# Spare words between the tile pools of a DiT block on one core: the same instructions at other SBUF addresses

## The chip, the core and the metric

The kernel runs on one core of one Trainium2 chip. TensorE (PE in the profile) multiplies; it reads both operands from SBUF and writes to PSUM. VectorE (DVE), ScalarE (ACT) and GpSimd (POOL) prepare operands and empty PSUM, and DMAs queued by SyncE (SP) bring weights from HBM. The metric is the device time of one execution in microseconds: 1252.46 us before (median of 3 runs, 1251.32 to 1253.43).

## What is computed

Two layers of a diffusion transformer over 512 latent tokens and 256 context tokens, 1024 wide. Layer 0 mixes tokens by pooling over windows, layer 1 by grouped-query attention (8 heads, 4 of keys and values). Each layer ends in a squared-ReLU MLP of width 4096. Cut to what matters:

```python
for i in range(DEPTH):                       # 2 layers
    sh1, sc1, g1, sh2, sc2, g2 = split(s_lat @ ada_w[i] + ada_b[i], 6)
    a_l = modulate(rms_norm(h_lat, norm_g[i, 0]), sh1, sc1)
    ...
    y_l = pool_mix(a_l, ...) if kind == 0 else attn_mix(a_c, a_l, ...)
    h_lat = h_lat + g1 * y_l
    m_l = modulate(rms_norm(h_lat, norm_g[i, 1]), sh2, sc2)
    h_lat = h_lat + g2 * (square(relu(m_l @ mlp_w1[i])) @ mlp_w2[i])
    ...                                      # the context alike in layer 0
return rms_norm(h_lat, final_g)
```

## The kernel before

**Arithmetic.** All large products are fp32r matmuls. To keep precision, each operand is split into a rounded part and the rest (`hilo`, L91 and L92: ACT copies the rounded part, DVE subtracts it from the source), and a product is three matmuls: high by high, high by low, low by high. A matmul has a *streamed* operand (256 or 512 columns of 4 bytes pass through the array) and *weights* (128 x 128, loaded before it; the profile calls the load PEld). The weights of the next matmul are loaded while the one before streams.

**Stages and lines.** Pooling and its mix (L641, L668); MLP of layer 0 over 16 chunks of 256 hidden columns; attention (projections L889, scores L967 and L968, values L998, output L1009); MLP of layer 1. In an MLP chunk the first product is either plain (`m1_chunk`, L376) or, from chunk 5 of layer 0 and chunk 4 of layer 1 on, by Strassen's scheme with seven half-sized products of 256 columns (`m1_strassen`, L444; its part for the context is L464). The second product is `m2_chunk`, L495: for each of 8 output blocks, six matmuls with 512 latent columns, and in layer 0 six with 256 context columns between them. So 14 chunks of layer 0 give 672 pairs of one 512-column and one 256-column matmul. Adaptive-norm parameters of layer 1 are summed by L232.

**Order.** The scheduler and two hand-ordered stretches set each engine's order; every engine works its queue in that order and waits by semaphores. The program is fully unrolled.

**Where tiles lie.** Pools are laid out in SBUF in the order in which they are opened, each tile rounded up to 32 bytes, one after another. What begins 32 bytes past a multiple of 128 at the start of a pool stays there for all its tiles, since the tiles are multiples of 128 bytes long and all slices that matmuls read start at multiples of 512 bytes. The table gives for each pool what matmuls read from it, and its start modulo 128 in the built program, before and after the change:

| pool | tiles that matmuls read | before | after |
| --- | --- | --- | --- |
| `const` | `ident`, `ones` | 0 | 0 |
| `big` | `act`, `m_hi`, `m_lo` (`a_m_hi`, `a_m_lo` in attention), `h_ctx` (also spare weights of Strassen in layer 1) | 32 | 0 |
| `wp` | `w`: weights, and streamed by the projections L889 | 32 | 32 |
| `mc` | `m_c`, `a_c`, attention's `q` and `o`, Strassen weights of layer 1 | 96 | 64 |
| `xs` (both layers) | `xs`: sums streamed by Strassen | 96 | 64 |
| `op` (layer 0) | `op`: Strassen weights | 96 | 32 |
| `kvp` | `k` (streamed), `v` (weights) | 96 | 32 |

So before, `act` and `w` are 0 apart modulo 128, as are `m_hi` and `w`, `xs` and `op`; `m_c` and `w`, `m_hi` and `op`, `act` and `v` are 64 apart. The pairs are read off the table the same way for any product.

Of the kernel before, what the change touches and what calls it, by code (L numbers as in the profile page):

```python
# [8 lines left out]
F32 = mybir.dt.float32  # L9
# [5 lines left out]
P = 128  # L15
# [32 lines left out]
def dit_block_kernel(ctx: ExitStack, tc: tile.TileContext, xT, cols, adab, adaw, w1, w2, wqkv, wo,  # L48
# [4 lines left out]
    def sb(stack, name, bufs):  # L53
        return stack.enter_context(tc.tile_pool(name=name, bufs=bufs))

    const = sb(ctx, "const", 1)
    big = sb(ctx, "big", 1)
    wp = sb(ctx, "wp", 4)
    rp = sb(ctx, "rp", 2)
    sc = sb(ctx, "sc", 4)  # L60
    sm = sb(ctx, "sm", 4)
    mc = sb(ctx, "mc", 5)
    raws = sb(ctx, "raws", 2)
    mm, aux = (ctx.enter_context(tc.tile_pool(name=n, bufs=b, space=bass.MemoryType.PSUM))
# [2 lines left out]
    scope = ExitStack()  # L67
# [2 lines left out]
    accp, rbp = (mc, "mc"), (rp, "r")  # L70

    acts2 = big.tile([P, 2, 4 * T], F32R, tag="act", name="act")
    uid = [0, 0]

    def new(p, shape, dt, tag, bufs=None):
        uid[0] += 1
        kw = {"bufs": bufs} if bufs else {}
        return p.tile(shape, dt, tag=tag, name=f"{tag}{uid[0]}", **kw)
# [38 lines left out]
    for u in range(0, 4, 2):  # L117
        pair = new(wp, [P, 2, 1024], F32, "w")
# [271 lines left out]
    def strassen_inputs(m, xs, tmp, cuts):  # L390


        def quarter(i, j):
            return [m[0][x][:, 4 * i : 4 * i + 4, 256 * j : 256 * j + 256] for x in range(2)]

        def total(dst, a, b, op):
            s, e = (new(tmp[0], [P, 4, 256], F32, tmp[1]) for _ in range(2))

            with tc.high_priority(offset=-BEHIND):
                for o, x in ((s, 0), (e, 1)):  # L400
                    dve.tensor_tensor(o, a[x].bitcast(F32), b[x].bitcast(F32), op=op)
                dve.tensor_tensor(s, s, e, op=ALU.add)
                hilo(dst[0], dst[1], s)

        b11, b12, b21, b22 = (quarter(i, j) for i in range(2) for j in range(2))
        b7, b6, b1 = ([t[:, x] for x in range(2)] for t in xs)
        sums = ((b7, b21, b22, ALU.add), (b6, b11, b12, ALU.add), (b1, b11, b22, ALU.add),
                (b12, b12, b22, ALU.subtract), (b21, b21, b11, ALU.subtract))

        def steps(todo):  # L410
            for x in todo:
                total(*x)
                yield
        return (b22, b12, b21, b11, b7, b6, b1), [steps(sums[i:j]) for i, j in zip((0,) + cuts, cuts + (5,))]
# [430 lines left out]
    def strassen0(m):  # L845
        nonlocal scope, praw, ada_acc, ada_r
        scope.close()
        scope = ExitStack()
        xsp, opp, rawp = sb(scope, "xs", 1), sb(scope, "op", 3), sb(scope, "pair", 1)
        xs = [xsp.tile([P, 2, 4, 256], F32R, tag=f"xs{i}", name=f"xs0{i}") for i in range(3)]  # L850
        praw = (raws, [P, 1024], F32, "raw")
        ada_acc = new(mc, [P, 2, 512], F32, "mc")
        ada_r = [xsp.tile([P, 512], F32R, tag=f"ada{x}", name=f"ada{x}") for x in range(2)]

        def op():
            got = {}

            def tile_of(n):
                for key, pair in (("a", (1, 2)), ("b", (7, 8))):
                    if n in pair:  # L860
                        if key not in got:
                            got[key] = new(wp, [P, 2, 2, 512], F32R, "w")
                        return got[key][:, n - pair[0]]
                return new(opp, [P, 2, 512], F32R, "op")
            return tile_of
        return STRASSEN_FROM[0], strassen_inputs(m, xs, (opp, "op"), (0, 1, 3)), lambda: new(rawp, [P, 2, 1024], F32, "pair"), op

    norm = mlp(0, m, T, last, between=between0, strassen=strassen0, acts=[act0], ws=ws, ahead=lambda: kws.extend(load_w(wqkv[u]) for u in range(2)))
    am_ = lazy_m("a", True)


    scope.close()
    scope = ExitStack()
    kvp = sb(scope, "kvp", 1)
    accp = rbp = (mc, "mc")
    kk = kvp.tile([P, 2, NKV, T], F32R, tag="k", name="k")
# [234 lines left out]
    scope = ExitStack()  # L1111
# [3 lines left out]
    xsp = sb(scope, "xs", 1)  # L1115
# [104 lines left out]
```

## Time and profile before

| | |
| --- | --- |
| median of 3 runs | 1252.46 us |
| the profiled execution | 1251.34 us, of which its span (first to last instruction) is 1249.2 us |
| granted TensorE clock, mean | 0.996 |
| HBM read | 135.25 MB, 110 GB/s over the span |

The page gives busy time by engine, then slices of the span, the chain that ended last, and groups of instructions. Of PE it gives a busy time of overlapped instructions: a matmul's own record (276 to 420 ns) is longer than the distance to the next one, since matmuls are pipelined. The distance between starts, which sets PE's pace, is the length of a stretch in which only one kind of matmul runs, divided by their number; a view of busy time in stretches (with a line as filter) gives both.

### The profile page before, as it was taken

How to read it: one execution, taken by the hardware profiler on the slowest of the kernel's cores; microseconds unless marked ns; L12 is line 12 of the kernel's file. 1: busy time of each engine (PE TensorE's matmuls, PEld its weight loads, DVE VectorE, ACT ScalarE, POOL GpSimd, SP SyncE). 2: the span in 40 equal slices, each digit the busy share in tenths (PEclk: the TensorE clock that was granted, in tenths of full speed). 3: DMA queues.
4: the chain of work that ended last, by engine and by line, in shares of the span. 5: the costliest groups of instructions: out<-in, count | busy, mean ns of one | idle time of the engine just before them, and what ended most of it. 6: DMA issues, size and time to landing. Idle time of an engine off the chain costs nothing.

```text
span 1249.2 us, 20001 instructions
## 1 busy us (share of the span) xinstructions
PE 1222.6 (98%) x7896; PEld 1080.2 (86%) x7896; DVE 1016.9 (81%) x1723; ACT 589.5 (47%) x1055; POOL 143.1 (11%) x129
## 2 busy tenths in 40 slices
PE   7999999999999999999999999999999999999996
PEld 4767888899999999999988888888988999999996
DVE  6564998888989788866888387879899989898986
ACT  6554533444444444334455264554565454545443
POOL 0300000122131322231012001000000000000002
PEclk9999999999999999999999999999999999999998
DMA  9866424333433333321122020211223332323201
GB/s 351 329 238 218 136 85 139 114 119 119 153 111 133 129 123 120 129 68 34 46 82 85 17 85 18 68 34 67 102 86 101 111 109 92 111 94 110 75 28 68
DMA packets 41310, 138.64 MB, mean 111 GB/s; under 512 B 4736, under 2 KB 8064, under 8 KB 41088
## 3 DMA queue, kind: packets, MB, share of 16 engines
q1 hardware_dynamic: 41216, 137.36, 32.0%
q8 instruction: 62, 1.02, 0.3%
q14 instruction: 32, 0.26, 0.1%
HBM read 135.25 MB, written 2.10 MB: 110 GB/s over the span
## 4 chain that ended last, share of the span: by engine, by line
PE 63%; issue 27%; DVE 4%; ACT 2%; DMA 2%; POOL 1%; SPq 0%; POOLq 0%; DVEq 0%; ACTq 0%
PE aux L495 10%; PE mm L495 10%; PE aux L889 7%; PE mm L444 5%; PE aux L464 5%; PE mm L376 5%; PE aux L444 4%; PE aux L1009 3%; PE aux L998 3%; PE mm L967 2%; DMA raw<-in_dram 2%; PE aux L192 1%; PE mm L668 1%; PE mm L764 1%; PE aux L988 1%
## 5 line engine op out<-in xcount | busy, mean ns | idle before, releaser
L495 PE MATMUL aux<-act,w 128*128 128x512 f32 (+1 forms) x1224 | 238.8, 346 | 0.3 <-DVE h_lat L353 0.2
L495 PE MATMUL mm<-act,w 128*128 128x512 f32 (+1 forms) x1224 | 237.2, 345 | 0.9 <-DVE h_lat L353 0.9
L495 PEld LDWEIGHTS mm<-act,w 128*128 128x128 f32 x1224 | 194.9, 189 | 31.6 <-DVE h_lat L353 1.1
L495 PEld LDWEIGHTS aux<-act,w 128*128 128x128 f32 x1224 | 194.7, 189 | 29.6 <-DVE h_lat L353 0.7
L92 DVE TENSOR_TENSOR w<-raw,w 128x1024 fp32r<-128x1024 f32 x106 | 129.3, 1224 | 28.4 <-ACT w L91 28.3
L91 ACT ACTIVATE w<-raw 128x1024 fp32r<-128x1024 f32 x106 | 110.2, 1056 | 77.6 <-PE aux L495 40.7
L353 DVE SCALAR_TENSOR_TENSOR h_lat<-aux,mod,h_lat 128x512 f32<-128x512 f32 (+1 forms) x180 | 122.4, 686 | 16.9 <-PE aux L495 14.2
L433 POOL TENSOR_TENSOR sc<-pair 128x512 f32<-128x512 f32 x55 | 80.0, 1462 | 314.2 <-DMA raw<-in_dram 106.7
L353 DVE SCALAR_TENSOR_TENSOR h_lat<-mm,mod,h_lat 128x512 f32<-128x512 f32 (+1 forms) x140 | 97.7, 700 | 5.5 <-PE mm L495 4.6
L376 PE MATMUL mm<-m_m_hi,w 128*128 128x512 f32 (+1 forms) x320 | 92.9, 352 | 0.2 <-ACT m_m_hi L91 0.2
L889 PE MATMUL aux<-w,a_m_hi 128*128 128x256 f32 (+1 forms) x384 | 86.3, 320 | 0.0
L224 DVE SCALAR_TENSOR_TENSOR mc<-raw,s_f,mc 128x512 f32<-128x512 f32 x112 | 83.7, 765 | 2.1 <-DMA raw<-in_dram 1.3
L444 PE MATMUL mm<-m_m_hi,mc 128*128 128x256 f32 x384 | 69.8, 281 | 0.0
L889 PEld LDWEIGHTS aux<-w,a_m_hi 128*128 128x128 f32 x384 | 63.4, 190 | 5.0
L376 PEld LDWEIGHTS mm<-m_m_hi,w 128*128 128x128 f32 x320 | 56.3, 189 | 10.2 <-ACT r L384 0.8
L464 PE MATMUL aux<-m_c,w 128*128 128x256 f32 x528 | 61.6, 276 | 0.0
L889 PE MATMUL aux<-w,a_m_lo 128*128 128x256 f32 (+1 forms) x192 | 61.2, 319 | 0.0
L464 PEld LDWEIGHTS aux<-m_c,w 128*128 128x128 f32 x528 | 60.8, 188 | 0.0
L444 PEld LDWEIGHTS mm<-m_m_hi,mc 128*128 128x128 f32 x384 | 59.4, 188 | 0.5
L291 POOL TENSOR_TENSOR sm<-sm,neghalf 128x2 f32<-128x2 f32 (+1 forms) x9 | 6.6, 738 | 443.4 <-DVE sm L289 443.4
L376 PE MATMUL mm<-m_m_lo,w 128*128 128x512 f32 (+1 forms) x160 | 56.1, 351 | 0.7 <-DVE m_m_lo L92 0.7
L444 PE MATMUL mm<-m_m_lo,mc 128*128 128x256 f32 x192 | 53.9, 281 | 0.0
(260 smaller groups left out, 2453.9 us busy)
## 6 DMA issues: line engine op xcount, KB each, us to landing
raw<-in_dram SPq DMA_DIRECT2D x155, 512.0 KB, 3.8
praw<-in_dram SPq DMA_DIRECT2D x34, 512.0 KB, 7.7
fin<-in_dram SPq DMA_DIRECT2D x24, 512.0 KB, 4.4
pair<-in_dram SPq DMA_DIRECT2D x22, 512.0 KB, 4.6
block<-in_dram SPq DMA_DIRECT2D x8, 512.0 KB, 7.2
h_lat<-in_dram SPq DMA_DIRECT2D x4, 512.0 KB, 6.3
w<-in_dram SPq DMA_DIRECT2D x4, 512.0 KB, 10.7
out_dram<-fin SPq DMA_DIRECT2D x8, 256.0 KB, 2.5
```

Source lines behind the costliest of these rows:

```text
L91: act.activation(hi, src, AF.Copy)
L92: lo_eng.tensor_tensor(lo, src, hi.bitcast(F32), op=ALU.subtract)
L224: dve.scalar_tensor_tensor(acc[:, s], w, scal, acc[:, s], op0=ALU.mult, op1=ALU.add)
L353: dve.scalar_tensor_tensor(h, ps, gate[:, dt, s : s + 1], h, op0=ALU.mult, op1=ALU.add)
L376: pe.matmul(ps[:, c0 : c0 + cn], lhs, ms(m, ax, k, c0, cn), start=k + wx + ax == 0, stop=k == KT - 1 and wx == 1)
L433: eng.tensor_tensor(t, x, y, op=how)
L444: pe.matmul(places[n], w[:, wx, k * P : k * P + P], inputs[n][ax][:, k], start=k + wx + ax == 0, stop=k == 3 and wx == 1)
L464: pe.matmul(pc[:, t * 256 : t * 256 + 256], ws[k // 4][:, wx, k % 4 * P : k % 4 * P + P], ms(m, ax, k, SEQ, CTX), start=k + wx + ax == 0, ...
L495: pe.matmul(ps, lhs, a[:, t, ax, c0 : c0 + n], start=t + wx + ax == 0, stop=t == 1 and wx == 1)
L889: pe.matmul(ps, lhs, ws[u][:, wx, o : o + width], start=k + ax + wx == 0, stop=k == KT - 1 and ax == 1)
L998: pe.matmul(po, v[:, vx, k, g * HD : g * HD + HD], pT[:, px, k, j0:j1].rearrange("p j q -> p (j q)"), start=k + vx + px == 0, stop=k == 5 ...
L1009: pe.matmul(ps, ws[j][:, wx, dt * P : dt * P + P], o[ax][:, j, c0 : c0 + n], start=j + wx + ax == 0, stop=j == 1 and ax == 1)
```

## The change

A helper `skip` opens a pool that holds one unused tile of n words. Five calls stand between the pools: 24 words (96 bytes) before `big`, 8 before `wp`, 24 before `mc`, 24 between `xs` and `op` in layer 0, and 24 before `kvp`. The Strassen scope of layer 1 gets none. The instructions of every engine, their order, shapes and semaphores are the same before and after; only SBUF addresses differ, as in the table above.

```diff
     const = sb(ctx, "const", 1)
+    def skip(stack, n):
+
+        uid[2] += 1
+        sb(stack, f"skip{uid[2]}", 1).tile([P, n], F32, tag="skip", name=f"skip{uid[2]}")
+
+    uid = [0, 0, 0]
+
+    skip(ctx, 24)
     big = sb(ctx, "big", 1)
+    skip(ctx, 8)
     wp = sb(ctx, "wp", 4)
     rp = sb(ctx, "rp", 2)
     sc = sb(ctx, "sc", 4)
     sm = sb(ctx, "sm", 4)
+    skip(ctx, 24)
     mc = sb(ctx, "mc", 5)
...
-    uid = [0, 0]
...
-        xsp, opp, rawp = sb(scope, "xs", 1), sb(scope, "op", 3), sb(scope, "pair", 1)
+        xsp = sb(scope, "xs", 1)
+        skip(scope, 24)
+        opp, rawp = sb(scope, "op", 3), sb(scope, "pair", 1)
...
     scope.close()
     scope = ExitStack()
+    skip(scope, 24)
     kvp = sb(scope, "kvp", 1)
```

## The prediction

> **What bounds the kernel now.** I read busy time by engine first, then who waited for whom on PE, then stretches with a single kind of matmul.
>
> ```profile
> PE 1222.6 (98%) x7896; PEld 1080.2 (86%) x7896; DVE 1016.9 (81%) x1723; ACT 589.5 (47%) x1055; POOL 143.1 (11%) x129
> PEclk9999999999999999999999999999999999999998
> PE mm L597 <- DMA h_lat<-in_dram: 6.8, 2, 6.3
> PE mm L967 <- ACT mc L91: 2.0, 4, 0.5
> PE 63%; issue 27%; DVE 4%; ACT 2%; DMA 2%; POOL 1%; SPq 0%; POOLq 0%; DVEq 0%; ACTq 0%
> ```
>
> PE is busy for 98% of the span at an ungated clock, its longest waits for others are 6.8 and 2.0 us, and in the chain that ended last "issue", time with no releaser in view, is on top of PE's own 63%. So the kernel lasts as long as PE's matmuls follow each other, and only a shorter distance between their starts can shorten it. Those distances, each from a stretch with one line alone (length, PE busy, number of matmuls):
>
> ```profile
> 255.64:261.07 5.43, 5.43 (x48) 1.00 0.13 53
> 783.77:789.52 5.75, 5.75 (x48) 1.00 0.01 3
> 974.53:980.18 5.65, 5.65 (x48) 1.00 0.32 97
> 931.01:941.88 10.87, 10.87 (x48) 1.00 0.60 175
> 963.65:974.52 10.87, 10.87 (x48) 1.00 0.45 153
> 773.42:777.61 4.19, 4.19 (x18) 1.00 0.00 0
> 140.41:157.04 16.63, 16.63 (x96) 1.00 0.39 127
> 157.05:165.38 8.33, 8.33 (x48) 1.00 0.05 5
> 563.27:580.21 16.94, 16.94 (x96) 1.00 0.00 1
> ```
>
> In this order they are: L464 (256 columns, `m_c` and `w`, 64 apart), 5.43 / 48 = **113.1 ns**; L889 (256, `w` and `a_m`, 0 apart), **119.8**; L444 (256, `m_hi` and `mc`, 64 apart), **117.7**; L376 in layer 1 (512, 0 apart), **226.5**; L495 in layer 1 (512, 0 apart), **226.5**; L998 (512, `act` and `v`, 64 apart), **232.8**; then pairs of 512 and 256 columns: L376 in layer 0, 16.63 / 48 = **346.5** a pair; two stretches of L495 in layer 0, 8.33 / 24 = **347.1** and 16.94 / 48 = **352.9**. The array does the same work in the first three, and DMA is quiet in the slowest of them (0.01), so it isn't DMA that slows it. What differs is which tiles are read. That is the reason to take addresses seriously; but the best 256-column stream is 64 apart, the best 512-column streams are 0 apart, so the trace gives no plain rule for the distance.
>
> **The change, part by part.** No instruction, wait or DMA is added, removed or moved, so there are three possible effects: on PE's distances, on other engines' durations, and on DMA landings. The counts come from the view that groups PE's instructions by line and shape:
>
> ```profile
> L495 PE MATMUL mm<-act,w 128*128 128x512 f32 x696 | 206.8, 393 | 0.0
> L495 PE MATMUL mm<-act,w 128*128 128x256 f32 x528 | 119.8, 281 | 0.9 <-DVE h_lat L353 0.9
> L444 PE MATMUL mm<-m_m_hi,mc 128*128 128x256 f32 x384 | 69.8, 281 | 0.0
> L464 PE MATMUL aux<-m_c,w 128*128 128x256 f32 x528 | 61.6, 276 | 0.0
> L376 PE MATMUL mm<-m_c,w 128*128 128x256 f32 x192 | 53.4, 278 | 0.0
> L444 PE MATMUL aux<-xs,op 128*128 128x256 f32 x396 | 50.0, 283 | 0.0
> L889 PE MATMUL aux<-w,a_m_hi 128*128 128x256 f32 x256 | 46.5, 283 | 0.0
> L889 PE MATMUL aux<-w,a_m_hi 128*128 128x512 f32 x128 | 39.8, 392 | 0.0
> L444 PE MATMUL aux<-xs,h_ctx 128*128 128x256 f32 x288 | 35.9, 279 | 0.0
> L1009 PE MATMUL aux<-mc,w 128*128 128x512 f32 x144 | 35.2, 392 | 0.0
> L444 PE MATMUL mm<-m_m_hi,op 128*128 128x256 f32 x176 | 34.7, 281 | 0.0
> L444 PE MATMUL mm<-m_m_hi,w 128*128 128x256 f32 x176 | 33.6, 283 | 0.0
> L998 PE MATMUL aux<-act,v 128*128 128x512 f32 x126 | 30.6, 395 | 0.0
> L968 PE MATMUL mm<-k,mc 128*128 128x256 f32 x96 | 27.0, 281 | 0.0
> L376 PE MATMUL mm<-m_m_hi,w 128*128 128x256 f32 x128 | 24.4, 286 | 0.2 <-ACT m_m_hi L91 0.2
> L889 PE MATMUL aux<-w,a_c 128*128 128x512 f32 x96 | 24.2, 400 | 0.0
> L444 PE MATMUL aux<-xs,mc 128*128 128x256 f32 x144 | 19.2, 283 | 0.0
> L1009 PE MATMUL aux<-mc,w 128*128 128x256 f32 x96 | 12.3, 281 | 0.0
> ```
>
> L495 has as many into `aux` as into `mm`; a `lo` operand is streamed half as often as its `hi`. I cost the case that **every pair now 32 or 96 apart runs at the best distance seen**, 113.1 and 226.5, 339.6 for a pair of both:
> - 672 pairs of L495 in layer 0, now between 347.1 and 352.9 (I take the middle, 350.0, having a stretch of each): 672 x 10.4 ns = 7.0 us.
> - 256-column streams 0 apart, 119.8: L889 384, L444 with `xs` and `op` 396 and with `m_hi` and `w` 264, L376 192, the rest of L495 (1,056 less 672) 384; 1,620 x 6.7 = 10.9 us.
> - Pairs of L376 in layer 0 (192), and those like them in the mix, the first chunk and the scores (48, 48, 96): 384 x 6.9 (346.5 less 339.6) = 2.6 us.
> - 512-column streams 64 apart at about 232.8: L998 126, L1009 144, L889 with `a_c` 96; 366 x 6.3 = 2.3 us.
> - 256-column streams 64 apart at about 117.7: L444 with `m_hi` and `op` 264, L1009 96; 360 x 4.6 = 1.7 us.
>
> Together **24.5 us**. Not in it: 528 of L464 and some 1,000 512-column matmuls of L495, L376 and L889, which run at the best distance already, and 1,008 of layer 1's Strassen products (`m_hi` with `mc`, `xs` with `mc` and `h_ctx`), which the change leaves 64 or 0 apart: there it doesn't do what its words say. Bounds of this unknown: below, the same streams could go to the slow distances (priced under the rivals, 15 us longer); above, they could beat 113.1 and 226.5 (41 us more).
>
> The trace shows 32 or 96 apart in one place only, `ada` streamed (96) while `ones` (0) is loaded:
>
> ```profile
> 471.28 0.88 PE L495 MATMUL aux<-act,w 128*128 128x512 f32 x4
> 471.99 0.63 PE L232 MATMUL aux<-ada,ones 128*128 128x512 f32 x2
> 472.46 1.10 PE L495 MATMUL mm<-act,w 128*128 128x512 f32 x5
> ```
>
> Two 512-column matmuls take 0.47 us, 235 each: no better than 64 apart. They stand alone amid pairs of L495, whose distances depend on what went before, so this weakens the forecast without deciding it.
>
> DVE, ACT and POOL read and write the moved tiles; I cost them at nothing, since all starts stay multiples of 32 bytes and PE's queue covers them. That cover is thinnest here (PE, PEld, DVE, ACT, POOL busy):
>
> ```profile
> 0.00:50.00 50.00, 40.72 (x268) 28.74 (x269) 33.04 (x94) 29.67 (x52) 8.21 (x14) 1.00 0.90 342
> 150.00:200.00 50.00, 50.00 (x289) 43.34 (x288) 48.67 (x65) 18.78 (x23) 1.30 (x1) 1.00 0.29 95
> 950.00:1000.00 50.00, 50.00 (x281) 43.85 (x281) 47.74 (x63) 25.24 (x36) 0.00 (x0) 1.00 0.34 114
> ```
>
> DVE is busy 48.67 of 50 us in one stretch, so PE can gain at most 1.3 there. The pairs of L495 gain 3%, 1.5 of 50: some 0.2 us comes back, which I leave out. DMA binds only in the first 50 us (0.90 busy); landings move from 96 to 64 modulo 128, and I take nothing, with 1 us (2% of that stretch) either way as an allowance of mine.
>
> The sum goes against the profiled execution: 1251.34 - 24.5 = 1226.8, and the median of the runs is 1.1 above that execution, so **1228**.
>
> **Rivals.**
> *Slower: the new distances are poor ones.* If 32 and 96 apart behave like `ada` and `ones`, the streams now at the best distance lose it: 1,008 of 512 columns (720 of L495, 96 of L376, 192 of L889) x 6.3 = 6.4 us; L464, 528 x 6.7 = 3.5; the pairs go to 352.9: 672 x 2.9 and 384 x 6.4 = 4.4; the 360 go to 119.8: 0.8. That is 15.1 us: 1268. It decides as soon as more is lost on L464 and layer 1's 512-column streams (9.9 us) than is won on the 256-column streams that are 0 apart (10.9 us). For it: those streams are at their best without the change.
> *Faster still: the start within 64 bytes counts.* The distances differ in steps, 119.8 - 113.1 = 6.7 and 232.8 - 226.5 = 6.3, and 16 columns (64 bytes) at 226.5 / 512 ns each last 7.1. So reads seem to go in pieces of 64 bytes. Before, every streamed fp32r tile starts 32 past a multiple of 64, so it may need one piece more; after, all but `w` and `k` start on one. Those are 6,174 matmuls (2,448 of L495, 672 of L376, 1,932 of L444, 528 of L464, 594 others) x 6.7 = 41 us, also in layer 1's Strassen, less about 2 us where DVE is full: 1228 - 41 + 2 = 1189. Against: no row shows an aligned stream.
> [...]
> *No change.* Distances may depend on something that the spare words do not alter, or gains and losses may cancel: 1252. For it: 0 and 64 apart each have fast and slow streams. Against: the rows above differ by tiles alone.
> [...]
>
> **How the numbers follow.** The forecast (gains of half to all of the 24.5 us or a little more) 0.42, 1220 to 1240; faster still 0.14; no change 0.13; slower 0.31. A measurement of this kernel can tell about 0.2%, 2.5 us, from no change. Faster is 0.56, same 0.13, slower 0.31. The range reaches from the rival below to the one above, 1190 to 1268; beyond its ends I leave about 1 in 10 on each side.
>
> **What would show it.** The same stretches after: L889 with 256 columns falling from 119.8 to about 113 and pairs of L495 from 350 to 340 bear the forecast out; L464 and layer 1's L495 must stay at 113 and 226.5. L444 with `m_hi` and `mc` is the test of the third case: it stays 64 apart and becomes aligned, so a fall below 113 there means alignment and not distance. L464 at 118 or more, or layer 1's L495 at 233, means the slower case. The forecast is wrong if PE's distances stay and DVE or DMA rows change instead.

## The result and the profile after

The changed kernel takes 1256.76 us (median of 4 runs, 1256.40 to 1259.26) beside 1251.89 us before (4 runs): ratio 1.0049, 95% interval 1.0037 to 1.0061. It is **0.5% slower**, some 5 us, where 24 us less were forecast. Ratios here and below leave out two executions at a much lower granted clock, one of `both` (0.848) and the profiled one of `placed` (0.557), whose distances are therefore not read.

The profiled execution has a span of 1254.3 us beside 1249.2. Three lines of its page, busy time by engine, TensorE's granted clock in slices, and the chain that ended last:

```profile
PE 1228.1 (98%) x7896; PEld 1079.9 (86%) x7896; DVE 1021.6 (81%) x1723; ACT 589.3 (47%) x1055; POOL 140.9 (11%) x129
PEclk9999999999999999999999999999999999999999
PE 64%; issue 28%; DVE 3%; DMA 2%; ACT 2%; POOL 1%; SPq 0%; POOLq 0%; DVEq 0%; ACTq 0%
```

PE has the same matmuls and is busy 5.5 us longer, and the shares of the chain are as before. The span understates the loss, though, because the granted clock differed in the opening. The first 100 us, before and after (length, PE busy and number of matmuls, clock, DMA share, GB/s):

```profile
0.00:100.00 100.00, 89.21 (x572) 0.98 0.81 302
0.00:100.00 100.00, 89.46 (x588) 1.00 0.80 302
```

At 1.00 in place of 0.98, 16 more matmuls are on record in the same time, and the stretch of L376 shown below starts at 138.66 us, where it started at 140.41 before. Ten profiled executions show the same: from 50 to 100 us the clock was 1.00, 0.97 or 0.93, and the first matmul of L376 started at 94.1 to 94.2, 95.7 to 96.6 and 97.2 to 97.5 us. From that stretch of L376 to the end of the span the changed kernel takes 1115.6 us beside 1108.8, so 6.8 us longer. The whole runs agree: executions of the unchanged kernel at a mean clock of 0.994 averaged 1253.2 us and those at 0.998 1249.8 (12 of each), while the three of the changed kernel at 0.998 took 1256.4 to 1257.1. At a like clock the change costs about 7 us.

So the loss lies where the prediction looked, in the distances between matmul starts. Here are the same stretches as in the prediction, in its order (start and end, length, PE busy and number of matmuls of that line alone, clock, DMA share, GB/s; lines stand 9 to 12 higher in the changed file):

```profile
254.50:260.13 5.63, 5.63 (x48) 1.00 0.10 41
785.15:790.75 5.60, 5.60 (x48) 1.00 0.01 3
977.43:983.08 5.65, 5.65 (x48) 1.00 0.37 103
932.64:943.84 11.20, 11.20 (x48) 1.00 0.59 183
966.24:977.43 11.19, 11.19 (x48) 1.00 0.41 143
774.72:778.91 4.19, 4.19 (x18) 1.00 0.00 0
138.66:155.50 16.84, 16.84 (x96) 1.00 0.40 126
155.50:163.97 8.47, 8.47 (x48) 1.00 0.06 11
564.02:580.97 16.95, 16.95 (x96) 1.00 0.00 1
```

Length by number gives, before and after (lines as before the change):

| stretch | distance modulo 128, before and after | ns before | ns after |
| --- | --- | --- | --- |
| L464, 256 columns | 64, 32 | 113.1 | 117.3 |
| L889, 256 | 0, 32 | 119.8 | 116.7 |
| L444 `m_hi` and `mc`, 256 | 64, 64 | 117.7 | 117.7 |
| L376 in layer 1, 512 | 0, 96 | 226.5 | 233.3 |
| L495 in layer 1, 512 | 0, 96 | 226.5 | 233.1 |
| L998, 512 | 64, 96 | 232.8 | 232.8 |
| L376 in layer 0, a pair | 0 and 64, 96 and 32 | 346.5 | 350.8 |
| L495 in layer 0, a pair | 0, 96 | 347.1 and 352.9 | 352.9 and 353.1 |

No stretch that is now 32 or 96 apart reaches 113 or 226, and the streams that ran at 113 or 226 before have lost that pace. Over all starts in the two traces: L495 in layer 1 costs 4.0 us more (672 matmuls, mean 227.2 and now 233.1 ns), L464 2.2 (528), the 512-column streams of L889 1.0 and of L376 in layer 1 0.6, L1009 0.5, L444 with `op` as weights 0.5, the context columns of L495 0.8. Gains are smaller: 1.1 us on the 256-column streams of L889, 0.7 on `xs` and `op`, 0.8 on the other 256-column streams that were 0 apart. These terms come to 7.0 us, the loss at a like clock.

### The profile page after: what moved, and what is told of

Read it like the earlier page. It is cut to its first block, busy times and chain, and to the rows that moved or that the text cites. A ratio compares the mean times of both kernels' runs of the same rounds, so it can differ in the third digit from the quotient of the medians.

```text
span 1254.3 us, 20001 instructions
## 1 busy us (share of the span) xinstructions
PE 1228.1 (98%) x7896; PEld 1079.9 (86%) x7896; DVE 1021.6 (81%) x1723; ACT 589.3 (47%) x1055; POOL 140.9 (11%) x129
## 4 chain that ended last, share of the span: by engine, by line
PE 64%; issue 28%; DVE 3%; DMA 2%; ACT 2%; POOL 1%; SPq 0%; POOLq 0%; DVEq 0%; ACTq 0%
PE aux L504 10%; PE mm L504 10%; PE aux L901 9%; PE mm L385 6%; PE aux L473 5%; PE mm L453 5%; PE aux L453 4%; PE aux L1021 3%; PE aux L1010 3%; PE mm L979 2%; PE aux L1000 1%; PE mm L773 1%; PE aux L201 1%; PE mm L980 1%; PE mm L677 1%
## 5 line engine op out<-in xcount | busy, mean ns | idle before, releaser
L362 DVE SCALAR_TENSOR_TENSOR h_lat<-aux,mod,h_lat 128x512 f32<-128x512 f32 (+1 forms) x180 | 122.8, 688 | 18.7 <-PE aux L504 15.1
L385 PE MATMUL mm<-m_c,w 128*128 128x256 f32 x192 | 53.8, 280 | 0.0
```

The lines of the kernel that those rows point to most:

```text
L362: dve.scalar_tensor_tensor(h, ps, gate[:, dt, s : s + 1], h, op0=ALU.mult, op1=ALU.add)
L385: pe.matmul(ps[:, c0 : c0 + cn], lhs, ms(m, ax, k, c0, cn), start=k + wx + ax == 0, stop=k == KT - 1 and wx == 1)
```

## The experiments

Three theories stood against each other. *Distance*: what counts is how far, modulo some power of two, the streamed columns begin from the weights that are loaded beside them. *Alignment*: what counts is where a streamed tile starts, within 64 bytes. *Neighbours*: DVE, ACT or DMA reach other addresses too, and disturb PE there.

**A ruler.** A kernel of fp32r matmuls alone, 48 to a stretch, with no other engine at work. It computes none of the block. Its core:

```python
for i in range(count):
    k, (wx, ax) = i // 3, PASSES[i % 3]
    m0 = ax * 2048 + k % 4 * 512 + mo       # start of the streamed columns, in words
    w0 = wx * 512 + k % 4 * 128 + wo        # start of the weights
    pe.matmul(ps[:, :n], wts[:, w0 : w0 + P], mov[:, m0 : m0 + n], start=i == 0, stop=i == count - 1)
```

> Nothing of the reference is computed: after a warm-up, 64 stretches of 48 matmuls each, 512 or 256 columns, three to a step (weights high twice, weights low once) as in the kernel, and nothing beside them. The start of the streamed tile is moved by 0 to 112 bytes in steps of 16 with the weights fixed at 0 modulo 128 (names ending in m), and then the weights with the streamed tile fixed (names ending in w); the list runs forward and then backward. Theory A, the distance modulo 128 between streamed tile and weights sets the pace, wherever they start: rows m and w of the same distance (taken modulo 128) agree; 0 apart gives about 226.5 ns at 512 columns and 120 at 256, 32 and 96 apart about 233 and 117.5, 64 apart about 233 and 113 or 118. Theory B, the start of the streamed tile within 64 bytes sets it: rows w with the streamed tile at 0 are all equal, and rows m are slower wherever the tile starts off a multiple of 64, by about 6.7 ns. Theory C, neither counts and the pace comes from other engines' traffic: all 512-column stretches within 1 ns of each other, and all 256-column ones too.

The view by stretches, with the stretch's own PSUM tile as filter: 512 columns with `mo` at 0, 32 and 64 bytes, then 256 columns at 0, 32, 64, 96 and 112 bytes, and last 256 columns with the streamed tile left at 0 and the weights moved by 64 (`wo`).

```profile
32.99:43.87 10.88, 10.88 (x48) 1.00 0.00 0
54.99:66.20 11.21, 11.21 (x48) 1.00 0.01 1
77.39:88.39 11.00, 11.00 (x48) 1.00 0.01 1
210.74:216.48 5.74, 5.74 (x48) 1.00 0.00 0
222.18:227.78 5.60, 5.60 (x48) 1.00 0.01 3
233.46:239.12 5.66, 5.66 (x48) 1.00 0.01 3
244.88:250.64 5.76, 5.76 (x48) 1.00 0.00 0
250.64:256.08 5.44, 5.44 (x48) 1.00 0.01 3
278.85:284.29 5.44, 5.44 (x48) 1.00 0.02 5
```

512 columns: 226.7 ns at 0 apart, 233.5 at 32, 229.2 at 64. 256 columns: 119.6 at 0, 116.7 at 32, 117.9 at 64, 120.0 at 96, 113.3 at 112. So PE alone, with DMA at a share of 0.00 to 0.02 in these stretches, shows the kernel's distances, and the neighbours' theory is not needed. Nothing is shorter than 226.7 and 113.3, however it starts.

With the streamed tile fixed, the pace changes with the weights' place too: 512 columns take 227.7 with the weights at 0, 233.1 at 32, 233.2 at 64 and 234.1 at 96. So the start of the streamed tile alone doesn't set it, against *alignment*. But of *distance* modulo 128 one expectation failed too: the two ways of being 64 apart differ, 229.2 with the streamed tile moved and 233.2 with the weights moved, and 117.9 and 113.3 for 256 columns. This is taken up below.

**Everything moved together.** Eight words before `big` move all later pools by 32 bytes and keep every distance among them.

```diff
+    skip(ctx, 8)
     big = sb(ctx, "big", 1)
```

> The kernel before with 8 spare words ahead of the pool big and no others: every tile behind it moves by 32 bytes, so that all distances between streamed tiles and weights stay as before while the streamed tiles now start on multiples of 64. Theory A (distance): the time of before, 1252 us within 2.5, L464's stretch at 113 and layer 1's 512-column L495 at 226.5. Theory B (start within 64 bytes): 6.7 ns less on some 6,900 matmuls, about 1206 us. A theory that other engines or DMA pay for the new addresses: 1257 as with the change, with PE's distances as before.

1251.25 us beside 1251.48, ratio 1.0002 (0.9991 to 1.0014). Its page:

```profile
PE 1224.1 (98%) x7896; PEld 1081.9 (86%) x7896; DVE 1018.8 (81%) x1723; ACT 589.1 (47%) x1055; POOL 141.8 (11%) x129
```

By all their starts, L464 stays at 113.3 and layer 1's L495 at 227.2, as in the kernel before. Alignment falls. In the changed kernel too, `m_hi` and `mc` became aligned, stayed 64 apart, and stayed at 117.7.

**The change in parts.** `big_only` has the spare words before `big` and `wp`, `mc_only` those before `mc` (with them the later pools move too).

```diff
+    skip(ctx, 24)                        # big_only
     big = sb(ctx, "big", 1)
+    skip(ctx, 8)                         # big_only
     wp = sb(ctx, "wp", 4)
...
+    skip(ctx, 24)                        # mc_only
     mc = sb(ctx, "mc", 5)
```

> The first two skips of the change alone (24 words ahead of big, 8 ahead of wp): act and m are 96 apart from w, w and a_m 32 apart; mc, op, xs, k and v start as before, so m_c and w stay 64 apart. Theory A: layer 1's 512-column L495 goes from 226.5 to 233 (672 x 6 ns = 4.0 us), L376 in layer 1 and L889 with 512 columns alike (1.6 us), against 256-column L889 and L444 with w, 120 to 117 (1.5 us), and the rest 0.9 us: in all 4 to 5 us longer, 1256 to 1257, with L464 still at 113. If mc carries the loss: 1252.

> The third skip of the change alone (24 words ahead of mc): mc and all pools behind it go to 64, so m_c and w are 32 apart, m_hi and op 32 apart, act and v 32 apart, while act and w, m and w, xs and op stay 0 apart. Theory A: L464 goes from 113.3 to 117.4 (528 x 4.1 = 2.2 us), L1009 and L444 with op add about 0.9: about 3 us longer, 1255, with layer 1's L495 at 226.5. If big carries the whole loss: 1252.

Ratios 1.0060 (1.0039 to 1.0080) and 1.0033 (1.0021 to 1.0045). Stretches of `big_only`, of L464, of layer 1's L495 and of L444 with `m_hi` and `mc`:

```profile
254.71:260.15 5.44, 5.44 (x48) 1.00 0.18 69
964.76:975.96 11.20, 11.20 (x48) 1.00 0.42 146
975.96:981.65 5.69, 5.69 (x48) 1.00 0.34 105
```

and the same three of `mc_only`:

```profile
256.63:262.26 5.63, 5.63 (x48) 1.00 0.14 55
967.90:978.79 10.89, 10.89 (x48) 1.00 0.47 161
978.79:984.54 5.75, 5.75 (x48) 1.00 0.33 103
```

Each part slows streams whose distance it alters: `big_only` L495 (233.3) and not L464 (113.3), `mc_only` L464 (117.3) and not L495 (226.9). Both slow `m_hi` and `mc` (118.5 and 119.8), which the whole change leaves at 117.7 since both tiles move; over their 576 matmuls that is 1.7 us for the two parts. It is one reason why the parts' losses (0.60% and 0.33%) add up to more than the whole (0.49%). Another is that only the whole change wins 0.7 us on `xs` and `op`. The rest of the difference was not traced to a line. The words before `op` and `kvp` were not tried alone.

**Pairs on the ruler.** Pairs of 512 and 256 columns with the streamed tile, the weights, or one of the two streams moved; and stretches in which every second matmul has both operands moved by 64 bytes, so that each stream is 0 apart from its own weights and 64 apart from the weights of the next.

> Again nothing of the reference is computed; stretches of 48 steps by the same scheme, now for what the first such run left open. (1) Which weights count. In the stretches named swapped, streamed tile and weights move together between 0 and 64 bytes from one matmul to the next, so that each matmul is 0 apart from its own weights and 64 apart from those being loaded for the next. If its own weights count: 226.7 ns at 512 columns and 120 at 256, as in the stretches named plain. If the weights loaded beside it count: 229 to 233 and 113 to 118. (2) Pairs of a 512-column and a 256-column matmul, as in layer 0's L495 and L376, at 0, 32, 64 and 96 apart in both, or with only one of the two moved: 0 apart 347 to 353 ns a pair as in the kernel before; if distances simply add up, 512 at 0 apart and 256 at 64 apart gives 226.7 + 113.3 = 340, and 32 or 96 apart in both gives 350 to 351. (3) Whether 64 apart at 256 columns runs at 113 or 118 by its sign (up: the streamed tile moved; down: the weights moved) or by what ran before it: by sign, both stretches of one sign agree after a 512-column and after a 256-column stretch; by history, they differ.

First 512 columns plain and with operands swapped to and fro, then 256 columns likewise, then pairs at 0 and 0 apart, and with the 512-column stream alone 64 apart:

```profile
254.39:265.28 10.89, 10.89 (x48) 1.00 0.01 2
265.28:276.39 11.11, 11.11 (x48) 1.00 0.00 0
276.39:282.14 5.75, 5.75 (x48) 1.00 0.02 4
282.14:287.77 5.63, 5.63 (x48) 1.00 0.00 0
36.23:53.18 16.95, 16.95 (x96) 1.00 0.00 0
220.94:237.43 16.49, 16.49 (x96) 1.00 0.00 1
```

226.9 becomes 231.5 and 119.8 becomes 117.3, though each stream's own weights are where they were: it is the load beside the stream that counts, that of the next matmul. And a pair takes 353.1 at 0 and 0 apart but 343.5 with its 512-column stream 64 apart, which alone is the worse place for 512 columns (229.2 against 226.7). With the 512-column stream 0 apart and the 256-column one 64, each at the place that suits it alone, a pair takes 346.7, and not the sum of 340. A pair has an optimum of its own. The third question of this run got no answer: 256 columns 64 apart took 117.8 whichever tile was moved and whichever of the two stretches ran before.

**Using it: three placements.** `placed` puts 256-column streams 64 apart and 512-column streams 0 apart, by spare words around `xs`, between `k` and `v`, and by a start 16 words into some `w` tiles. `pairs` puts the latent columns of `act` in layer 0 64 apart, the context columns 0. `both` joins them.

```diff
-        t = new(wp, [P, 2, 1024], F32R, "w")                     # placed
+        t = new(wp, [P, 2080], F32R, "w")[:, off : off + 2048].rearrange("p (x n) -> p x n", x=2)
...
-    acts2 = big.tile([P, 2, 4 * T], F32R, tag="act", name="act") # pairs
+    acts2 = big.tile([P, 2, 4 * T + 32], F32R, tag="act", name="act")
+    lay = [16]                           # 0 from attention on
...
+        a, o = acts2[:, uid[1] % 2], lay[0]
+        lat, ct = a[:, o : o + 4 * SEQ], a[:, o + 4 * SEQ + 16 : o + 16 + 4 * T]
```

> Edit: the kernel before, with 64 bytes of distance (modulo 128) given to 256-column streams that were 0 apart, and 0 to 512-column streams that were 64 apart; order and instructions as before. 256 columns: xs on op (396), act on w in both tails (336), w on a_m (384), the first chunk of layer 1 (192), 1,308 together; 512 columns: act on v (126), o on w (144). Distance theory, by the ruler and the traces so far: 64 apart gives 256 columns 117.8 ns or 113.3 in place of 119.8, that is 2.6 or 8.5 us; 0 apart gives 512 columns 226.7 in place of 233.1 (v) and 230.1 (o), 0.8 and 0.5 us. So 3.9 to 9.8 us less than before: 1242 to 1248 us, and L464 and layer 1's L495 stay at 113.3 and 227.2. Rival (the pace belongs to the pair of tiles or to what else reads SBUF at that time, and moving them is neutral): 1252 us and the old distances on these lines.

> Edit: in layer 0, the latent columns of act begin 64 apart from w and the context columns stay 0 apart (latent and context columns of act are laid out one after the other with 64 spare bytes between); in layer 1 both are as before. m1_done of layer 0's first five chunks issues two instructions where it had one for the rounded part and for the rest. Distance theory by the ruler of pairs (343.3 ns for a pair of 512 columns 64 apart and 256 columns 0 apart): 672 pairs of L495 fall from about 350.7 to 343.3, 5.0 us, and 48 pairs of the mix (L668) another 0.4: about 1246.5 us. Rival 1 (each stream has its own best distance, whatever runs before it: 512 columns lose up to 6.4 ns when 64 apart): pairs of 352 or more and 1253 to 1256 us. Rival 2 (the ruler's pairs do not carry over into the kernel, where DVE, ACT and DMA read and write SBUF beside PE): 350 a pair and 1252 us.

> Edit: the two kernels above in one (the last chunk of layer 0 keeps its weights where they were, so that its 256-column latent streams are 64 apart by act's place). Distance theory: the gains add, 3.9 to 9.8 and 5.4 us: 1237 to 1243 us. If only one of the two edits does what the theory says, this run has the time of that one.

Ratios 0.9975 (0.9965 to 0.9985), 0.9990 (0.9980 to 0.9999) and 0.9981 (0.9972 to 0.9991): the gains are real, smaller than expected, and do not add. Part of where `pairs` lost its gain shows in layer 1, three chunks of L495 one after the other, whose `act` buffers alternate:

```profile
1004.05:1015.21 11.16, 11.16 (x48) 1.00 0.00 0
1025.02:1035.92 10.90, 10.90 (x48) 1.00 0.00 0
1045.84:1057.00 11.16, 11.16 (x48) 1.00 0.00 0
```

232.5, 227.1, 232.5. All are 0 apart modulo 128, but in `pairs` a buffer of `act` is 97 x 128 bytes long, so every second one is 128 apart **modulo 256**. That costs 1.8 us over layer 1. In `placed` and `both`, `w` tiles of 65 x 128 bytes do the same, and a chunk mixes both kinds (in `both` these three chunks take 232.1 to 232.3). A second thing shows one line earlier, in `xs` and `h_ctx` (256 columns, at one distance throughout) of three chunks:

```profile
980.50:983.22 2.72, 2.72 (x24) 1.00 0.12 44
1001.22:1004.05 2.83, 2.83 (x24) 1.00 0.12 49
1022.30:1025.02 2.72, 2.72 (x24) 1.00 0.27 110
```

113.3, 117.9, 113.3: at the same addresses, by turns, as the buffer of the L495 before was 128 or 0 apart. That suggested a memory of what ran before.

**Modulus and memory on the ruler.**

> A third kernel of matmul stretches alone, 48 a stretch, in two sweeps of opposite order; it computes none of the block. Streams of 512 (wide) and of 256 columns (short) at distances 0, 32, ... 480, 512 and 1024 bytes from the weights (letters a to r); a 256-column stretch 64 (then) or 192 apart (down) behind a 512-column stretch 0, 32, 64, 128 or 192 apart (enter, again); and pairs of 512 and 256 columns at (0,0), (64,0), (64,128), (192,0), (192,128), (128,0), (0,128), (64,256), (320,0), letters a to i. Theory 'modulo 128': wide_e, wide_i, wide_m, wide_q, wide_r (0 modulo 128) all 226.7, the other letters repeat with period 4, and pairs a to i depend on their distances modulo 128 alone (b to e, h and i alike, f and g like a). Theory 'modulo 256' (in the pairs kernel, layer 1's 512-column streams took 227 ns when act was 0 or 256 apart from w and 232.6 when 128 apart): wide_e and wide_m (128, 384) 232 to 233, wide_a, wide_i, wide_q, wide_r 226.7; pair b 343.3, c and d about 347.0. Theory of memory (in the pairs kernel xs on h_ctx, at one distance, ran at 113.3 and 117.8 by turns, as the act buffer before it was 128 or 0 apart): then_four and down_four 113.3, then_zero and down_zero 117.8, and some letters differ between the sweeps; without memory, all five 'then' are alike and the sweeps agree.

512 columns at 0, 32, 64, 96, 128 and 256 bytes; then 256 columns at 64 in the first sweep (behind a stretch 32 apart) and in the second (behind one 96 apart); then 256 columns at 192 behind a 512-column stretch 0 apart, and behind one 128 apart; last, pairs at (0, 0) and (64, 0):

```profile
37.51:48.39 10.88, 10.88 (x48) 1.00 0.00 0
48.39:59.59 11.20, 11.20 (x48) 1.00 0.00 0
59.59:70.59 11.00, 10.99 (x48) 1.00 0.01 1
70.59:81.80 11.21, 11.21 (x48) 1.00 0.00 0
81.80:93.00 11.20, 11.20 (x48) 1.00 0.01 1
126.62:137.51 10.89, 10.88 (x48) 1.00 0.00 0
248.92:254.58 5.66, 5.66 (x48) 1.00 0.00 0
942.81:948.25 5.44, 5.44 (x48) 1.00 0.00 0
367.58:373.24 5.66, 5.66 (x48) 1.00 0.01 3
468.05:473.50 5.45, 5.45 (x48) 1.00 0.00 0
506.98:523.63 16.65, 16.65 (x96) 1.00 0.00 0
523.63:540.14 16.51, 16.51 (x96) 1.00 0.00 1
```

The 512-column stream takes 226.7 at 0 and at 256 apart, 233.3 at 32 and at 128, 229.2 at 64, 233.5 at 96. All letters of one half of the scale repeat in the other (32 and 288, 64 and 320, and so on): for stretches of 512 columns alone the modulus is 256. It also gives what modulo 128 left open. Weights moved by 64 on the first ruler are 192 apart, where this ruler has 233.1; and the swapped stretch of 512 columns meets weights 64 and 192 apart by turns, 229.1 and 233.1 with a mean of 231.1, and took 231.5.

In the kernel it holds for 512 columns as well. Taken modulo 256, the addresses of the built programs move L495 and L376 in layer 1 from 0 to 224 apart (226.5, then 233.1 and 233.3; this ruler has 226.7 and 233.1), L998 from 192 to 224 (232.8 both times; 233.1 for both) and L1009 from 64 to 160 (mean 230.1, then 233.7; 229.1 and 234.2). So "64 apart" in the tables above joins two distances, 64 and 192, that differ for 512 columns. For 256 columns the fit is looser: `m_hi` and `mc` went from 192 to 64 (117.7 both times; 117.8 and 117.9 here), but L464 went from 64 to 160 and took 117.3, where this ruler has 118.6. And the two buffers of `pairs` put the pairs of L495 at (64, 128) and (192, 0), not at (64, 0). This ruler has 346.7 and 346.5 for these two, and the kernel took 347.0: the rest of the gain that `pairs` lacked, 672 x 3.7 = 2.5 us.

At 64 apart, 256 columns take 117.9 or 113.3 by what came before, at 192 likewise. Not all went as that theory had it: behind a stretch 192 apart a 256-column stretch 64 apart took 113.3 as well, behind 128 apart it did not. Nor do distances modulo 256 settle a pair: one at (64, 0) took 343.9, as on the ruler before (343.5), but at (64, 256) and (320, 0), the same modulo 256, pairs took 351.6 and 351.7, and pairs at (0, 0) took 347.0 here and 353.1 on the ruler before. Whether that is a longer period or the memory is open.

**One tile moved in the kernel.** `xs_only` moves `xs` of layer 0, and nothing else, to 64 apart from `op`. `placed_far` is `pairs` with buffers of 98 x 128 bytes, so that both lie alike modulo 256, with `xs` 64 apart from `op`, `v` 0 apart from `act`, and the last two chunks of layer 1 64 apart. `keep_xs` is that kernel without the moves of `xs` and `op`.

```diff
+        skip(scope, 16)                                          # xs_only
-        xsp, opp, rawp = sb(scope, "xs", 1), sb(scope, "op", 3), sb(scope, "pair", 1)
+        xsp = sb(scope, "xs", 1)
+        skip(scope, 48)                                          # xs_only
+        opp, rawp = sb(scope, "op", 3), sb(scope, "pair", 1)
...
+    acts2 = big.tile([P, 2, 4 * T + 64], F32R, tag="act", name="act")   # placed_far, keep_xs
+        lat, ct = a[:, o : o + 4 * SEQ], a[:, 4 * SEQ + 64 :]
...
+    skip(scope, 48)
+    v = sb(scope, "vp", 1).tile([P, 2, 6, NKV * HD], F32R, tag="v", name="v")
```

> Edit: the kernel of pairs with both act buffers at the same place modulo 256 (64 apart from w for latent columns of layer 0, 0 for its context columns, 0 in layer 1 but for its last two chunks, whose 256-column streams are 64 apart), xs 64 apart from op in layer 0 and v 0 apart from act. The w tiles stay where they were. Theory 'modulo 256': pairs of L495 at 343.3 as on the ruler, 720 x 7.5 = 5.4 us; xs on op 396 x 2.0 or 6.5 = 0.8 or 2.6; layer 1's tail 192 x 2.0 or 6.5 = 0.4 or 1.2; v 126 x 6.4 = 0.8: 7.4 to 10.0 us, 1241.5 to 1244 us; layer 1's L495 at 227 for both buffers. Theory 'modulo 128': pairs at 347.0 as in the pairs kernel, 2.7 us, and the rest the same: 1244.5 to 1247 us. Rival (placement moves streams between states that the neighbours set, and one gain is lost on the next line): 1249 to 1252 us.

> Edit: the kernel before with xs alone moved, in layer 0, by 64 bytes (16 spare words before it, 48 behind it, so that op and all others keep their place modulo 256): xs is 64 apart from op in place of 0; no other pair of tiles changes. Theory of distance alone: xs on op (396) falls from 119.6 to 117.8 or 113.3, 0.7 or 2.5 us, and L464, which runs behind it on tiles that keep their places, stays at 113.3: 1248.7 to 1250.5 us beside 1251.2. Theory of distance with memory (placed_far: L464 at 117.8 behind xs on op that was no longer 0 apart): L464 goes to 117.8 in its eleven chunks, 528 x 4.5 = 2.4 us: 1251.1 to 1252.9 us.

> Edit: the kernel of placed_far with xs and op where they are before the change. Theory of distance with memory: L464 back at 113.3 (528 x 4.5 = 2.4 us less than placed_far), xs on op back at 119.6 (396 x 2.0 = 0.8 us more), m_hi on op (264) back at 117 (0.7 us more): about 1248.5 us. Theory of distance alone (L464 at 117.8 in placed_far had another cause): L464 stays there and the time rises to about 1250.9 us.

`xs_only`: ratio 1.0009 (0.9998 to 1.0019), no gain. L464, whose own tiles didn't move (113.1 before):

```profile
257.25:262.90 5.65, 5.65 (x48) 1.00 0.10 41
```

117.7. All eleven Strassen chunks show it: 2.3 us lost there against 0.6 won on `xs` and `op`. `placed_far`, ratio 0.9988 (0.9979 to 0.9997), has L464 at 117.8 too, and its 1249.39 us are what its rival had foreseen, a gain lost on the next line; `keep_xs` undoes that and is at **1246.35 us, ratio 0.9959 (0.9945 to 0.9973)**, faster than both kernels of this study. Its L464; layer 1's L495; L998; and two stretches of layer 0's pairs:

```profile
255.97:261.41 5.44, 5.44 (x48) 1.00 0.09 36
960.44:971.32 10.88, 10.88 (x48) 1.00 0.47 160
770.67:774.77 4.10, 4.10 (x18) 1.00 0.00 0
157.69:165.93 8.24, 8.24 (x48) 1.00 0.05 7
561.13:577.61 16.48, 16.48 (x96) 1.00 0.00 1
```

113.3, 226.7, 227.8, and 343.3 a pair in both stretches, where the kernel before has 347.1 and 352.9. Over all starts of L495 the pairs' mean falls from 350.8 to 345.0: 672 x 5.8 = 3.9 us. `v` gives 126 x 5.0 = 0.6 and the last 256-column streams of layer 1 0.7. Together that is about the 5.1 measured (0.41% of 1251.6). It is 2.1 us better than expected: half of that lies in the pairs, at 346.5 in `placed_far` and 345.0 here, although the two kernels have them at the same distances.

## Why the prediction was wrong

- *PE's distances alone set the time.* Right from the first MLP on: the terms by line come to 7.0 us, and that part of the span is 6.8 us longer. The opening moved too, by 1.75 us the other way, with the granted clock.
- *The distances depend on which tiles are read, so on addresses.* Right: the ruler shows them with nothing beside, and the two parts of the change each move their own lines. What a stream takes depends on the weight load beside it: with PE alone at work, 512 columns took 226.7 ns at 0 apart and 233.5 at 32, and in the swapped stretches 226.9 became 231.5 with each stream's own weights left where they were.
- *"Every pair now 32 or 96 apart runs at the best distance seen."* **This step failed.** 32 and 96 apart are poor places for 512 columns: 233.1 to 233.3 in the kernel, 233.3 to 233.5 on the ruler. For 256 columns they are middling: 116.7 to 120.0. The best distances had been seen at 0 (512 columns) and at 64 (256) only; no row placed them at 32 and 96. The one row with such a distance, 235 a matmul for `ada` and `ones`, was set aside as weak, and pointed the right way. Behind it stood a second slip: distances were sorted modulo 128, where 512-column streams have a period of 256 (226.7 ns at 0 and 256, 233.3 at 128), so that streams 64 and 192 apart counted as one kind.
- *The terms.* Instead of gaining 7.0 us, the 672 pairs lost a little (mean 350.8 to 352.2); the 1,620 256-column streams that were 0 apart gained 2.6 instead of 10.9; the 512-column streams 64 apart and the 256-column streams 64 apart lost about 1 together instead of gaining 4.0; the 384 other pairs lost some 0.5 instead of gaining 2.6. One starting figure was off as well: L1009 was taken at 232.8 and had a mean of 230.1.
- *The slower rival.* Its mechanism is what happened, and its point of decision held: lost on L464 and the 512-column streams at their best 7.8 us (2.2 + 4.0 + 1.0 + 0.6), won on the 256-column streams 0 apart 2.6. Its 15.1 us was too much: it gave L464 the worst distance (119.8; it took 117.3), it had the pairs lose 4.4 us (they lost about 1), and it left out the 2.6 won.
- *Alignment* and *no change* are refuted: the first by `shift_all` (1.0002), by the ruler's stretches with the weights moved and by `m_hi` and `mc` at 117.7, the second by the result.
- *What the sum could not know:* L464 is at 113 behind `xs` on `op` 0 apart and at 117.7 behind the same streams 64 apart (`xs_only`). A distance read off one stretch is not a property of its two tiles alone.

## What to carry to other kernels

Where TensorE is busy throughout, divide the length of stretches with one kind of matmul by their number, and compare equal shapes: a spread of some per cent at one shape (here 113.1 to 119.8 ns for 256 columns) is worth looking for in addresses. Measure the candidates of distance by themselves before you place anything, since the best of the places seen says nothing about a place not seen (here 233.1 ns where 226.5 was forecast); and after a move read the stretch behind the moved one too (L464 went from 113.1 to 117.7 ns when `xs` was moved). Compare whole times only at a like granted clock, for here 0.994 against 0.998 (1253.2 and 1249.8 us) is worth half of what the change costs. Here fp32r streams of 512 columns ran best with their weights 0 apart modulo 256 (226.7 ns); those of 256 columns reached 113 at 64, 112 and 192 apart, but at 64 and 192 only behind some stretches, with 118 behind others; and alternations of both had a third optimum (343.5 and 343.9 a pair on two rulers with the 512-column stream alone 64 apart).

## What the runs showed of the hardware that was not expected

- The pace has a period of 256 bytes in the distance between a streamed tile and the weights loaded beside it: 226.7 ns at 0 and 256, 233.3 at 128, for 512 columns. Alternating pairs of 512 and 256 columns did not keep to it (343.9 at (64, 0), 351.7 at (320, 0)).
- It has a memory: the same 256-column stretch, at the same addresses and distances, took 113.3 or 117.8 ns depending on the stretches before it, and kept that for all its 24 to 48 matmuls. Which stretch leaves which pace behind was not settled.
- No stretch of fp32r came below 226.7 ns for 512 columns or 113.3 for 256, at a granted clock of 1.00 with PE alone at work.
